# Last rows in blocks of 32, with narrower final matmuls, in a 2-D prefix-sum diagonal kernel

## The chip, the cores and the metric

One core of one Trainium2 chip. The metric is the device time of one execution in microseconds (us); lower is better. Executions of one kernel are compared with those of the other on the same chip.

## The reference

```python
B, H, W = 4, 4224, 4224                      # x: fp32
ps = np.cumsum(np.cumsum(x, axis=1), axis=2)
diag = np.diagonal(ps, axis1=1, axis2=2)
return np.cumsum(diag, axis=1).astype(np.float32)
```

All of x (285 MB) must be read; the output is small. An element counts once for every place of the diagonal at or beyond both its row and its column. Rows are summed on all engines, and weighted sums over the rows then give the output.

## The kernel before

Loads are issued by GpSimd, with a cast to bf16. VectorE masks and sums, ScalarE sums pieces of rows, TensorE adds columns and folds pieces of rows (with an identity as weights) into PSUM. The last 384 rows of the last matrix are done at the end: 256 rows "part a" in two cuts, then 128 rows "part b" in three cuts of columns. This is the tail that the change concerns:

```python
        acuts = [(1536, N - HC), (0, 1536)]          # part a, 256 rows
        bcuts = [(2432, TB), (640, 2432), (0, 640)]  # part b, 128 rows
        # ... loads are issued here, some 50 us ahead ...
        fold_in(fold_a, part_a, c0, cp, 256)         # second cut of part a, TensorE
        for h in range(2):
            act_sum(asum[:, h, 3:4], part_a[:, h, cp:c1])   # ScalarE
        row_sums(asum[:, :, 4], fold_a)              # VectorE
        row_sums(arows, asum)

        shares = [(768, 512), (768, 512), (0, 320)]
        for i, ((c0, c1), (wp, wa)) in enumerate(zip(bcuts, shares)):
            fold_in(fold_b, part_b, c0, c0 + wp, 256, start=i == 0)
            act_sum(tsum[:, n : n + 1], part_b[:, c0 + wp : c0 + wp + wa])
            # ... VectorE sums the rest of the cut, and at i == 2 fold_b ...
            if i == 0:
                matmul(fin_b, arows[:, 0:1], weights[:, 2 * P : GW], start=True)
                # ... three more of arows into fin_b and fin_a ...
        row_sums(ttot, tsum)
        matmul(fin_b, ttot, weights[:, 0:P])
        # ... two additions into yl, two stores ...
```

TensorE's records come in the order of the program: the folds of the first cut (660.49 us) go ahead of the matmuls of arows (661.37). And the waits of TensorE and VectorE in this tail are on data (the longest are 1.22 us of TensorE for ttot and 0.94 of VectorE for a landing).

## Time and profile before

| | before |
|---|---|
| time, first three runs | 668.81 us (668.69 to 669.55) |
| span of the profiled run | 667.0 us |
| load engines | 90% or more busy in 39 of 40 slices |
| VectorE, TensorE, ScalarE busy | 50%, 32%, 21% |
| last landing of part b to the issue of the last store | 1.62 us |
| that issue to the end of the span | 1.97 us |

The span is the profiler's, from the first to the last instruction; the time includes some 1.7 us more (668.75 us for the profiled run). The prediction below shows the lines of the page and of the timeline that carry this. A timeline line has start, duration, engine, source line, operation, output<-input, shape and count, and in brackets how long the engine had been idle and what ended that.

### The profile page before, as it was taken

What the parts mean: (1) busy time and instruction counts of PE and PEld (TensorE: products, weight loads), DVE (VectorE), ACT (ScalarE), POOL (GpSimd) and SP (SyncE); (2) the same over time, 40 slices, a digit from 0 to 9 for tenths busy, and PEclk for the clock granted to TensorE, in tenths of its full rate; (3) what the DMA queues carried; (4) which work ended last, traced back from release to release, by engine and by line L of the source; (5) the groups of instructions that cost most, each with busy time, mean ns of one, the idle gap of its engine ahead of it and who ended that gap; (6) DMA issues with size and microseconds to landing.
All of it is one profiled execution on the core that took longest, in us unless ns stands there. A gap on an engine that the chain in (4) does not pass through costs nothing.

```text
span 667.0 us, 2828 instructions
## 1 busy us (share of the span) xinstructions
PE 215.1 (32%) x967; PEld 97.2 (15%) x967; DVE 336.3 (50%) x376; ACT 140.1 (21%) x225; POOL 27.0 (4%) x56
## 2 busy tenths in 40 slices
PE   0071522403118254140321633504032254250426
PEld 0030211101003022010110311201011122120202
DVE  2043617366924351745883415266398241635687
ACT  0001120406300103040630020304063002030436
POOL 5000000000000000000000000000000000001000
PEclk9995857666558586665655957567565586765758
DMA  9999999999999999999999999999999999999997
GB/s 203 219 219 219 218 219 219 217 217 216 208 215 219 219 219 217 216 219 219 219 219 215 216 211 217 220 219 216 216 216 219 220 215 218 216 215 219 216 207 144
DMA packets 7384, 143.25 MB, mean 215 GB/s; under 512 B 669, under 2 KB 842, under 8 KB 1866
## 3 DMA queue, kind: packets, MB, share of 16 engines
q0 software_dynamic: 7008, 142.47, 99.7%
q1 hardware_dynamic: 362, 0.61, 0.3%
q8 instruction: 7, 0.11, 0.1%
q14 instruction: 7, 0.06, 0.0%
HBM read 285.47 MB, written 0.07 MB: 428 GB/s over the span
## 4 chain that ended last, share of the span: by engine, by line
another core or an unknown queue 42%; DVE 25%; PE 23%; DMA 5%; issue 4%; DVEq 0%; POOLq 0%
PE d L198 23%; DVE acc L215 17%; DVE mu L218 7%; DMA strip<-in_x_dram 5%; PE fold L198 1%; DVE pu L215 0%; DVE c L397 0%; DVE c L218 0%; DVE tsum L215 0%; DVE acc L301 0%; DVE acc L304 0%; PE carry_ps L198 0%; DVE rows L331 0%; DVEq L218 0%
## 5 line engine op out<-in xcount | busy, mean ns | idle before, releaser
L218 DVE SCALAR_TENSOR_TENSOR mu<-strip,um 128x768 bf16<-128x768 bf16 (+1 forms) x129 | 110.7, 908 | 314.4 <-DMA strip<-in_x_dram 222.3
L198 PE MATMUL d<-strip,sel 128*11 128x384 bf16 x603 | 140.0, 406 | 344.4 <-DMA strip<-in_x_dram 344.4
L210 ACT ACTIVATE dump<-strip 128x416 bf16<-128x416 bf16 (+8 forms) x112 | 128.4, 1146 | 523.2 <-DMA strip<-in_x_dram 520.2
L215 DVE TENSOR_REDUCE acc<-strip 128x6 f32<-128x4608 bf16 (+6 forms) x23 | 195.9, 8518 | 0.0
L198 PEld LDWEIGHTS <-sel 128*11 128x11 bf16 x849 | 86.1, 101 | 526.3 <-issue 488.4
L198 PE MATMUL d<-mu,sel 128*11 128x384 bf16 x243 | 59.7, 355 | 67.5 <-DVE mu L218 67.4
L75 POOL DMA_DIRECT2D strip<-in_x_dram x24 | 16.5, 687 | 555.5 <-DVE acc L215 414.5
L210 ACT ACTIVATION_READ_ACCUMULATOR dump<-strip 128x1 f32 x112 | 20.9, 186 | 0.0
L218 DVE DVE_READ_ACCUMULATOR mu<-strip,um 128x1 f32 x129 | 10.6, 82 | 0.0
L198 PE MATMUL d<-ident,rows 128*11 128x128 f32 x24 | 5.2, 378 | 16.5 <-DVE rows L340 16.5
L198 PE MATMUL fold<-strip,ident_h 128*128 128x480 bf16 (+1 forms) x14 | 4.3, 458 | 8.4 <-DMA strip<-in_x_dram 8.4
L198 PE MATMUL d<-halves,rows 128*11 128x64 f32 x48 | 5.7, 304 | 0.0
L198 PEld LDWEIGHTS d<-halves,rows 128*11 128x11 f32 x48 | 5.1, 136 | 2.1 <-issue 2.1
L198 PEld LDWEIGHTS d<-ident,rows 128*11 128x11 f32 x24 | 2.6, 118 | 18.2 <-DVE rows L340 11.5
L215 DVE TENSOR_REDUCE pu<-d 11x1 f32<-11x384 f32 x4 | 2.2, 546 | 5.5 <-PE d L198 5.5
L397 DVE TENSOR_TENSOR_SCAN c<-ones_row,carry,c 11x384 f32<-11x384 f32 x4 | 4.0, 1006 | 0.1
L397 DVE TENSOR_TENSOR_SCAN c<-ones_row,carry,d 11x384 f32<-11x384 f32 x4 | 4.0, 1001 | 0.1
L198 PEld LDWEIGHTS <-ident_h 128*128 128x128 bf16 x20 | 2.2, 112 | 12.2 <-issue 11.8
L215 DVE TENSOR_REDUCE parts<-strip 128x3 f32<-128x3072 bf16 x1 | 3.4, 3350 | 0.0
L198 PE MATMUL d<-hmu,sel 128*11 128x384 bf16 (+2 forms) x3 | 0.7, 286 | 6.7 <-DVE hmu L218 6.7
L372 POOL DMA_DIRECT2D strip<-in_x_dram x2 | 1.4, 716 | 29.2 <-DVE acc L215 29.2
L215 DVE TENSOR_REDUCE tsum<-strip 128x1 f32<-128x384 bf16 (+2 forms) x3 | 1.7, 568 | 0.9 <-DMA strip<-in_x_dram 0.9
(78 smaller groups left out, 36.0 us busy)
## 6 DMA issues: line engine op xcount, KB each, us to landing
strip<-in_x_dram POOLq DMA_DIRECT2D x19, 6336.0 KB, 69.6
strip<-in_x_dram POOLq DMA_DIRECT2D x5, 3168.0 KB, 55.3
strip<-in_x_dram POOLq DMA_DIRECT2D x1, 1080.0 KB, 45.3
strip<-in_x_dram POOLq DMA_DIRECT2D x1, 768.0 KB, 48.2
head<-in_x_dram SPq DMA_DIRECT2D x1, 528.0 KB, 3.9
strip<-in_x_dram POOLq DMA_DIRECT2D x1, 448.0 KB, 51.1
strip<-in_x_dram POOLq DMA_DIRECT2D x1, 416.0 KB, 49.5
strip<-in_x_dram POOLq DMA_DIRECT2D x1, 160.0 KB, 51.4
```

The lines of the kernel that those rows point to most:

```text
L75: nc.gpsimd.dma_start(out=o, in_=x[b, r0 : r0 + f * P, :].rearrange("(p f) w -> p f w", f=f))
L198: nc.tensor.matmul(o, lhsT=lhsT, rhs=rhs, start=start, stop=False, skip_group_check=True)
L210: nc.scalar.activation(out=dump[:, :w], in_=src, func=ACT.Copy, accum_out=acc)
L215: nc.vector.reduce_sum(out=acc, in_=src, axis=AX.X)
L218: nc.vector.scalar_tensor_tensor(out=o, in0=i, scalar=1.0, in1=m, op0=ALU.mult, op1=ALU.mult, accum_out=acc,)
L372: nc.gpsimd.dma_start(out=part_a[:, :, c0:c1], in_=src_a[:, :, c0:c1])
L397: nc.vector.tensor_tensor_scan(out=c12[:, i, :], data0=ones_row, data1=src, initial=carry[:, i : i + 1], op0=ALU.mult, op1=ALU.add,)
```

## The change

The intent is to shorten what follows the last landing. Part b comes in blocks of 32 rows, each row spread over four partitions. The last block then concerns only 32 places of the output, so the last matmuls and the last addition cover 32 instead of 128 columns, and each partial sum goes into PSUM by a matmul of its own, without an addition of sums first.

```diff
+    quarter = consts.tile([R, P], FP32, name="quarter")      # R = 32; mask made on GpSimd
+    w4_ps = psum_s.tile([P, P], FP32, name="fold")
+    matmul(w4_ps, quarter, weights[:R, :P], start=True)       # weights for quarter rows
...
-            bcuts = [(2432, TB), (640, 2432), (0, 640)]
-            for c0, c1 in bcuts:
-                nc.gpsimd.dma_start(out=part_b[:, c0:c1], in_=x[b, TB:N, c0:c1])
-            fold_a = psum_s.tile([P, 2, 256], FP32, name="fold_a")
+            for sb, c0, c1 in ((0,0,CB), (1,0,CB), (2,0,CB), (3,0,bcut), (3,bcut,CB)):  # CB = 1024, bcut = 640
+                r0 = TB + sb * R
+                nc.gpsimd.dma_start(out=part_b[:, sb, c0:c1],
+                    in_=x[b, r0 : r0 + R, :TB].rearrange("r (k c) -> r k c", k=4)[:, :, c0:c1])
+            fold_a = psum_s.tile([P, 2, P], FP32, name="fold_a")
...
+        weigh(arows[:, 0:1], weights, 0, fins, start=True)    # fins: fin_a 256, fin_m 96, fin_e 32 columns
+        weigh(arows[:, 1:2], weights, P, fins)
+        weigh(dtot, weights, M0, fins)                        # eight matmuls, ahead of all folds of part b
+        for sb, (wp, wa) in enumerate([(512, 512), (384, 384), (384, 320)]):
+            # folds of 128 columns into fold_b[:, sb], act_sum, and at sb == 0:
+                finish(fin_a, 0, M0)                          # VectorE addition
+            # VectorE sums the rest of the block
+        row_sums(bsum[:, :, 2], fold_b)
+        row_sums(btot, bsum)
+        for sb in range(3):
+            weigh(btot[:, sb : sb + 1], weights4, M0 + sb * R, fins)
+        # last block: four sums (two ScalarE, two VectorE) into esum
+        for k in range(4):
+            weigh(esum[:, k : k + 1], weights4, E0, fins)
+        finish(fin_m, M0, E0)       # store of 352 places
+        finish(fin_e, E0, GW)       # store of 32 places
```

## The prediction

> **What bounds the kernel now.** I read the page first: the load row by slices, then the chain that ended last.

> ```profile
> span 667.0 us, 2828 instructions
> DMA  9999999999999999999999999999999999999997
> GB/s 203 219 219 219 218 219 219 217 217 216 208 215 219 219 219 217 216 219 219 219 219 215 216 211 217 220 219 216 216 216 219 220 215 218 216 215 219 216 207 144
> another core or an unknown queue 42%; DVE 25%; PE 23%; DMA 5%; issue 4%; DVEq 0%; POOLq 0%
> ```

> The 16 DMA engines are at 90% or more in 39 of 40 slices and move about 217 GB/s of bf16, so the kernel is a stream of loads, and VectorE at 50% or TensorE at 32% follow it. The 42% of "another core or an unknown queue" is waiting for that stream. What a change of the last 128 rows can move is only what follows the stream: the last slice. So I then read the timeline from 658 us. Its columns are start, duration, engine, line, operation, output<-input, shape, and in brackets the idle time before and what ended it.

> ```profile
> 658.49 0.81 PE L198 MATMUL fold_a<-strip,ident_h 128*128 128x512 bf16 x3 [0.38 <-DMA strip<-in_x_dram]
> 660.30 0.66 DVE L215 TENSOR_REDUCE asum<-fold_a 128x2 f32<-128x512 f32 x1
> 660.49 0.49 PE L198 MATMUL fold<-strip,ident_h 128*128 128x256 bf16 x3 [1.19 <-DMA strip<-in_x_dram]
> 661.06 0.16 DVE L215 TENSOR_REDUCE arows<-asum 128x2 f32<-128x10 f32 x1
> 661.37 0.60 PE L198 MATMUL fin_b<-weights,arows 128*1 128x128 f32 x4 [0.39 <-DVE arows L215]
> 661.80 0.81 PE L198 MATMUL fin_a<-weights,arows 128*1 128x256 f32 x4
> 662.62 0.69 DVE L215 TENSOR_REDUCE tsum<-strip 128x1 f32<-128x512 bf16 x1 [0.94 <-DMA strip<-in_x_dram]
> 663.22 0.41 DVE L215 TENSOR_REDUCE tsum<-fold 128x1 f32<-128x256 f32 x1
> 663.51 0.47 ACT L210 ACTIVATE dump<-strip 128x320 bf16<-128x320 bf16 x1
> 663.55 0.47 DVE L215 TENSOR_REDUCE tsum<-strip 128x1 f32<-128x320 bf16 x1
> 664.13 0.16 DVE L215 TENSOR_REDUCE ttot<-tsum 128x1 f32<-128x8 f32 x1
> 664.35 0.38 PE L198 MATMUL fin_b<-weights,ttot 128*1 128x128 f32 x2 [1.22 <-DVE ttot L215]
> 664.77 0.28 DVE L446 TENSOR_TENSOR yl<-fin_b,c 1x128 f32<-1x128 f32 x1 [0.16 <-PE fin_b L198]
> ```

> The landings show as the starts after waits: the last cut of the rows before (a1) at 658.49, then the three cuts of the last rows at 660.49, 662.62 and about 663.5. From the last landing the path is: VectorE sum 0.47, ttot 0.16, final matmul 0.38, addition 0.28, store. The store is issued at 665.07 (its own record) and the span ends at 667.04, so 1.97 us follow that issue. The quantity to predict is when the last store is issued: 665.07 before.

> [...] packets of 1280, 3072, 3328 and 3584 bytes last 117, 248, 265 and 284 ns, about 24 ns plus 13.7 bytes per ns. [...] the trace has no row of bf16 matmuls of 128 columns with full weights (256 columns: 107 ns from start to start)[...]. [...] Here each VectorE record starts after the one ahead of it, even ttot, which waited.

> **Part by part.**
> Start: a mask of 32x128 on GpSimd (memset and two selects, some 0.7 us by its like there), one small matmul, one copy, one memset. GpSimd's constants end at 10.79 us and VectorE's at 8.8; the first strip lands at 34.6. Hidden, 0.

> Loads: three transfers become five; each partition takes 2048+2048+2048+1280+768 bytes instead of 3328+3584+1280. Each engine serves 8 partitions, so it has 16 packets more at 24 ns: 0.38 us, perhaps 0.34 because packets overlap a little (the DMA share reads 1.06 there). By the 8 packets of each engine, the landings should be at about a1 + 1.3, 2.6, 3.9, 4.8 and 5.4 us: 659.8, 661.1, 662.4, 663.3, 663.9. The last transfers reuse semaphores of earlier loads, which landed by 634.7, some 27 us before; the stream does not run dry.

> fold_a halves from 2x256 to 2x128 columns. TensorE streams the same columns (six matmuls of 256 instead of three of 512). Its VectorE sum drops from 0.655 to 0.414, the time of the 128x256 PSUM sum at 663.22: minus 0.24. arows is done at 660.98 instead of 661.22, and its first matmul can start at 661.13 instead of 661.37.

> Final matmuls of arows: eight logical fp32 matmuls now stand ahead of the folds of the last rows on TensorE; before, the first fold went ahead of them. Each is two passes of 0.84 ns per column (256 columns start 215 ns apart, 128: 108, 64: 54). Up to the one that completes fin_a: 2x(256+96+32)x0.84 = 0.645, then 0.108 to its second pass, plus 0.27 of that pass: done at 662.15. The other four, 2x256x0.84 = 0.43, let folds start at 662.42. [...] Between 0.054 each and 0.107 each this is 663.2 to 663.7.

> VectorE is the new path. Straight after arows its program has the addition that finishes fin_a, which waits for TensorE until 662.2; before, that addition filled the gap after ttot. VectorE thus stands idle 1.2 us, although the second block has landed at 661.1. Then: fin_a 0.32 (0.40 less 0.08 of overlap, as successive records show), bsum of 256 elements 0.32, bsum of 320 elements 0.39: 663.23. The sum of the fold (3x128 columns, 0.53 between 0.41 at 256 and 0.655 at 512) waits for TensorE: 663.47 to 664.00. Then 0.10 for its result, btot started at 664.10, esum of 320 at 664.18, esum of 256 at 664.57, ended at 664.98 (0.40). Next 0.05 to TensorE, two passes of 32 columns (0.03 and 0.19 to drain): 665.25; addition of 32 places 0.19: 665.48; store issued 665.50. The addition for fin_m and the first store fit beside the last matmuls.

> Sum: 665.50 - 665.07 = plus 0.43 us. What the change saves behind the last landing (ttot gone, addition of 32 instead of 128 places: 0.28 to 0.19; matmul record 0.38 to 0.22) is real but stands behind a VectorE that is late: the last block has landed 0.7 us before VectorE gets to it.

> **Rivals.**
> 1. The intended gain shows. If VectorE were free at 663.9, the path would be sum 0.40, matmul 0.27, addition 0.23, issue: about 664.9, minus 0.2 us, so 668.6. For it: the removed tail lies on the chain. Against it: the early fin_a addition and 1.5 us of VectorE work between the last fold and the last sum.
> 2. The loads become the bound: small pieces land later than I reckon. Against: packets' own durations give only 0.38 us, and 0.7 us of slack stand behind it. Were they 1.2 us late, the end would be 0.5 us later still, 669.7.
> 3. TensorE becomes the bound: weight loads of the folds not hidden, or its clock halved. The clock reads 1.00 from 656 to 664. [...]

> **Range and chances.** 668.81 + 0.43 gives 669.2. Runs of before spread over 0.86 us, and the working can err by some 0.6 us: 668.4 to 670.1. Two per cent is 13.4 us, twice the whole time after the last fold started; nothing touches the stream of loads ahead of that. Within 2%: 0.985, faster 0.005, slower 0.01.

> **What would show it.** In the changed profile: the load row as before; VectorE idle for over 1 us before the addition into yl from fin_a, released by TensorE; the fold sum at about 663.5 waiting for TensorE; the two esum sums on VectorE back to back without a wait for a load. Wrong if the last esum starts after a wait for a load (rival 2), if the sum of fold starts without waiting or well before 663.4 (towards rival 1), or if the stream before 650 us moves.

The sum came to plus 0.43 us (665.50 for 665.07). Passages that no trace of this case shows are cut where marked, and terms of that sum are among them: what one of the ten folds takes, and with it when they end and how much the third rival costs. What stays is the range for their end, 663.2 to 663.7, an estimate from the trace: ten times what 128 columns take at 0.42 ns (256 start 107 ns apart) or at twice that (480 start 400 ns apart at 650.4, where the clock reads 0.50), and some 0.2 us for the last to end (records of 256 columns last 270 ns). The sum took an end between the two, so that the fold sum starts at 663.47. From the range alone the estimate is plus 0.2 to 0.7. That VectorE keeps the order of its program rests on the trace: the addition of fin_a starts at 664.21, after ttot, though TensorE was done with fin_a at 662.62. In the records packets of 1280, 3072, 3328 and 3584 bytes last 116, 248, 267 and 286 ns, and each cut of part b is 128 packets (8 for each of the 16 load engines if they share evenly, as the forecast took it).

## The result

The changed kernel took 670.75 us (median of 6, 669.8 to 671.77); the kernel before, on the same chip, 669.28 (median of 6, 668.69 to 670.25). The ratio is 1.0021 with a 95% interval of 1.0008 to 1.0034. (Ratios here are the mean time of one kernel's fast runs over the mean of the other's in the same rounds, so not quite the ratio of the medians.) The change is slower by some 1.4 us where I had said 0.43, and 670.75 lies outside the range of 668.4 to 670.1. Both times are within 2% of each other, as forecast.

The page of the changed kernel, its first line and the load row: the stream is as it was.

```profile
span 669.0 us, 2916 instructions
DMA  9999999999999999999999999999999999999996
```

The timeline of the changed kernel, the tail, to set beside the lines of the prediction:

```profile
659.20 0.81 PE L214 MATMUL fold_a<-strip,ident_h 128*128 128x256 bf16 x6 [0.82 <-DMA strip<-in_x_dram]
660.57 0.39 DVE L236 TENSOR_REDUCE asum<-fold_a 128x2 f32<-128x256 f32 x1
661.18 0.16 DVE L236 TENSOR_REDUCE arows<-asum 128x2 f32<-128x10 f32 x1 [0.22 <-ACT dump L231]
661.40 0.66 PE L214 MATMUL fin_a<-weights,arows 128*1 128x256 f32 x2 [1.38 <-DVE arows L236]
...
662.29 0.61 PE L214 MATMUL fin_a<-weights,arows 128*1 128x128 f32 x2
...
662.95 0.41 DVE L480 TENSOR_TENSOR yl<-fin_a,c 1x256 f32<-1x256 f32 x1 [1.60 <-PE fin_a L214]
...
663.69 1.25 PE L214 MATMUL fold<-strip,ident_h 128*128 128x128 bf16 x10
...
664.98 0.56 DVE L236 TENSOR_REDUCE bsum<-fold 128x3 f32<-128x384 f32 x1 [0.90 <-PE fold L214]
665.64 0.16 DVE L236 TENSOR_REDUCE btot<-bsum 128x3 f32<-128x9 f32 x1
665.72 0.80 DVE L236 TENSOR_REDUCE esum<-strip 128x1 f32<-128x320 bf16 x2
...
666.83 0.18 DVE L480 TENSOR_TENSOR yl<-fin_e,c 1x32 f32<-1x32 f32 x1
667.05 0.25 SPq L516 DMA_DIRECT2D out_dram<-yl  x1
```

The shape is what I predicted: VectorE waits 1.60 us for fin_a, then 0.90 us for the folds, then works without a wait to the end. But TensorE is far slower than reckoned: from the first matmul of arows at 661.40 to the end of the folds at 664.94 it takes 3.54 us, where the range in the forecast gives 2.1 to 2.6. The next view says why. It gives for two stretches of 3.4 us the busy time (and number of instructions) of PE, PEld, DVE, ACT and POOL, then the granted TensorE clock, the share of the load engines and GB/s; first the kernel before, then the changed kernel:

```profile
658.40:661.80 3.40, 1.73 (x10) 0.84 (x10) 3.14 (x5) 2.59 (x6) 0.00 (x0) 1.00 0.98 189
661.80:665.20 3.40, 1.69 (x11) 0.62 (x8) 2.17 (x6) 1.28 (x4) 0.00 (x0) 1.00 0.08 13
```

```profile
658.40:661.80 3.40, 1.22 (x8) 0.66 (x9) 2.64 (x5) 2.49 (x6) 0.00 (x0) 1.00 1.10 200
661.80:665.20 3.40, 3.14 (x25) 2.35 (x23) 1.35 (x4) 2.24 (x10) 0.00 (x0) 0.50 0.23 40
```

The two profiles differ by 2.0 us of span. The last cut of part a lands at 658.49 before and at 659.20 after, 0.71 us later; from that landing to the issue of the last store it takes 6.58 us before and 7.85 after. So 1.27 us belong to the tail, and 0.71 to the stream of loads ahead of it. This is a comparison of one profile with one; the experiments show how little that is.

### The profile page after: what moved, and what is told of

Its sections match the earlier page's. It is cut to its first block, busy times and chain, and to the rows that moved or that the text cites. A ratio compares the mean times of both kernels' runs of the same rounds, so it can differ in the third digit from the quotient of the medians.

```text
span 669.0 us, 2916 instructions
## 1 busy us (share of the span) xinstructions
PE 216.3 (32%) x1005; PEld 99.9 (15%) x1005; DVE 336.8 (50%) x380; ACT 140.9 (21%) x229; POOL 28.0 (4%) x61
## 4 chain that ended last, share of the span: by engine, by line
another core or an unknown queue 37%; DVE 24%; PE 22%; DMA 13%; issue 4%; ACT 0%; DVEq 0%; POOL 0%; POOLq 0%; ACTq 0%
PE d L214 21%; DVE acc L236 16%; DMA strip<-in_x_dram 13%; DVE mu L239 6%; DVE pu L236 0%; PE fin_m L214 0%; DVE c L239 0%; ACT dump L231 0%; PE fold L214 0%; DVE acc L327 0%; DVE acc L324 0%; PE fin_a L214 0%; PE fin_e L214 0%; PE carry_ps L214 0%
## 5 line engine op out<-in xcount | busy, mean ns | idle before, releaser
L214 PE MATMUL d<-strip,sel 128*11 128x384 bf16 x603 | 138.6, 403 | 334.8 <-DMA strip<-in_x_dram 334.8
L231 ACT ACTIVATE dump<-strip 128x416 bf16<-128x416 bf16 (+9 forms) x114 | 129.1, 1132 | 523.1 <-DMA strip<-in_x_dram 520.2
L214 PE MATMUL fold<-strip,ident_h 128*128 128x128 bf16 (+1 forms) x18 | 4.6, 440 | 7.6 <-DMA strip<-in_x_dram 7.6
```

Source lines behind the costliest of these rows:

```text
L214: nc.tensor.matmul(o, lhsT=lhsT, rhs=rhs, start=start, stop=False, skip_group_check=True)
L231: nc.scalar.activation(out=dump[:, :w], in_=src, func=ACT.Copy, accum_out=acc)
```

## The experiments

**Theory, as first put.** The change moves the eight matmuls of arows ahead of the folds of part b. That leaves TensorE idle between the last fold of part a and arows (659.85 to 661.40), the clock drops at its next step, and folds that stand behind a slow stream of matmuls come late. **Rivals.** VectorE is blocked by the early addition of fin_a, as the prediction had it; the two further loads land late; the stream is delayed; the amount of work on VectorE is the bound. The first half of the theory (the new order is needed for the drop) fell in the course of the runs; the second half (what a drop costs) stood.

A look is one profiled run. The table has every look, the two first profiles included, ordered by where the clock's next possible step falls, with the three looks with fillers at the end. "Landing" is the start of the first fold on the last cut of part a. "Step" is how long after it the step of the 3.41 us grid falls (of the steps on that grid, the one from 1.0 to 4.4 us after the landing). "Tail" is from the landing to the issue of the last store.

| look | landing, us | step, us after it | clock halved there | tail, us |
|---|---|---|---|---|
| no folds, second | 658.61 | 1.46 | yes | 6.62 |
| changed, third | 660.12 | 1.63 | yes | 7.77 |
| before, fourth (state unknown) | 658.57 | 2.11 | yes | 7.57 |
| changed, fin_a's addition last | 659.60 | 2.11 | yes | 8.25 |
| before, arows first, third (unknown) | 659.98 | 2.16 | yes | 7.83 |
| changed, fold first, second | 658.45 | 2.33 | yes | 7.67 |
| changed, first | 659.20 | 2.60 | yes | 7.85 |
| before with the start part, second | 658.96 | 2.72 | yes | 7.28 |
| before, second | 658.47 | 3.09 | no | 6.58 |
| changed, second | 659.29 | 3.58 | no | 6.60 |
| before, third (unknown) | 658.52 | 3.67 | no | 6.58 |
| before, first | 658.49 | 3.93 | no | 6.58 |
| changed, fold first | 659.59 | 3.97 | no | 6.72 |
| no folds | 658.59 | 3.99 | no | 6.18 |
| before, arows first | 658.51 | 4.07 | no | 6.58 |
| before with the start part | 659.51 | 4.24 | no | 6.60 |
| before, arows first, second (unknown) | 658.60 | 4.27 | no | 6.58 |
| no folds, with fillers | 660.43 | 1.16 | no | 6.20 |
| changed, with fillers | 659.09 | 2.76 | no | 6.45 |
| before, with fillers | 658.86 | 2.85 | no | 6.58 |

**The changed kernel again** (no edit).

> The changed kernel once more, to see how much of its tail depends on where the TensorE clock's steps fall. In its first profile the clock went to 0.5 at 661.80 us, in the middle of the matmuls of arows, and the time from the end of arows (VectorE) to the issue of the last store was 5.71 us (kernel before: 3.85 us). Clock theory: where the clock stays at 1.00 through this stretch, that time is about 4.4 us, as the prediction worked it out; where it drops again, 5.5 to 5.8. Rival (order on VectorE and TensorE alone): 5.6 to 5.8 whatever the clock. Time against before: 1.002 again.

Its clock stayed at 1.00 to the end. From the end of arows to the last store 4.31 us instead of 5.71, and the tail was 6.60 us, that of the kernel before within 0.02. 670.06 us against 668.98 (ratio 1.0008, 0.9992 to 1.0024). From its timeline:

```profile
662.70 0.41 DVE L480 TENSOR_TENSOR yl<-fin_a,c 1x256 f32<-1x256 f32 x1 [1.13 <-PE fin_a L214]
663.04 0.73 PE L214 MATMUL fold<-strip,ident_h 128*128 128x128 bf16 x10
663.82 0.56 DVE L236 TENSOR_REDUCE bsum<-fold 128x3 f32<-128x384 f32 x1
...
665.89 0.25 SPq L516 DMA_DIRECT2D out_dram<-yl  x1
```

The same program, with the same order on every engine, has tails 1.25 us apart. The clock is the only difference found that can make the slow one slow (its arows even ended 0.15 us sooner after the landing). So the late folds of the first profile are put down to the clock, and at full clock the change costs 0.02 us in the tail. One thing more shows here: at full clock VectorE waits 1.13 us for fin_a, but not for the folds. What holds it up then is the early addition of fin_a, as the prediction had it; the folds hold it up only when the clock is halved.

**Fillers.** Matmuls whose result nobody reads:

```diff
         fold_in(fold_a, part_a, c0, cp, P)
+        warm = psum_d.tile([NG, GW], FP32, name="d")
+        for i in range(8):
+            matmul(warm, sel[:, :NG], part_a[:, 0, i * 8 : i * 8 + GW], start=i == 0)
```

> Eight idle-filling matmuls of 384 columns into an accumulator that nobody reads stand between the last fold of part a and the matmuls of arows, where TensorE was idle for 1.6 us. Clock theory: the clock stays at 1.00 to the end, the folds end some 1.2 us earlier (1.5 instead of 3.3 us after the first matmul of arows, less a little), and from the end of arows to the last store it takes about 4.4 us instead of 5.71: about 1.2 us less in the median. Rival (order alone): 5.6 us or more, the time unchanged.

From its timeline:

```profile
659.83 1.47 PE L214 MATMUL d<-strip,sel 128*11 128x384 bf16 x8
...
661.28 0.59 PE L214 MATMUL fin_a<-weights,arows 128*1 128x256 f32 x2
...
662.69 0.73 PE L214 MATMUL fold<-strip,ident_h 128*128 128x128 bf16 x10
663.46 0.56 DVE L236 TENSOR_REDUCE bsum<-fold 128x3 f32<-128x384 f32 x1
...
665.54 0.25 SPq L519 DMA_DIRECT2D out_dram<-yl  x1
```

The step fell at 661.85 us, all but where the clock dropped in the first profile (661.80), and it did not drop. (Counted from the landing it fell at 2.76, at the border of the looks that dropped, so the place alone might have spared it. By the rule below it would not have: in its stretch 2.49 us of columns streamed, far over the 1.28 of any that dropped, and 1.29 of them, 8 x 384 columns at 0.42 ns, are the fillers' own. An estimate from these: without them 1.2, just on the side that drops.) Ten folds take 0.73 us instead of 1.25, and from arows to the last store 4.31. With more work on TensorE the tail is 1.40 us shorter than in the first profile. 668.93 us against 668.98 for the kernel before (ratio 0.9994, 0.9981 to 1.0008). Against the changed kernel in the same job the mean is 0.84 us less (668.96 to 669.80, 95% interval 0.2 to 1.5; a comparison picked afterwards), so here the gain seems to show in the time too.

**The addition of fin_a moved.** `finish(fin_a, 0, M0)` goes from `sb == 0` to just ahead of `finish(fin_m, M0, E0)`.

> Only the addition that finishes fin_a moves on VectorE, from straight after arows to ahead of that of fin_m. My prediction's theory (VectorE blocked by that addition sets the end): VectorE sums the second block at about its landing, but fin_a's 0.32 us comes back on the end; gain at most 0.2 us. TensorE theory (the ten folds behind the matmuls of arows set when the fold sum can start): the fold sum starts as late as before, about 3.6 us after the end of arows when the clock drops, and the end is 0.3 us later than in the changed kernel. Neither makes it faster by over 0.2 us.

The clock dropped at 661.71. VectorE summed the second block at 662.07, at its landing, but the sum of the folds started as late as ever, 3.78 us after arows, and the addition's time came on top: 6.11 us from arows to the last store, 0.4 more than 5.71 where I had 0.3. The rival of the prediction (VectorE held up by that addition) is refuted while the clock is halved; the folds set the end. (669.1 us against 668.98; ratio 1.0006, 0.999 to 1.0022; its profiled run was the slowest of its six, 671.52.)

**Folds of the first block first.**

```diff
-        weigh(arows ...); weigh(arows ...); weigh(dtot ...)      # ahead of the loop
+            if sb == 0:  weigh(arows ...); weigh(arows ...); weigh(dtot ...)   # after the folds of block 0
```

> Only TensorE's order: the four folds of the first block go ahead of the matmuls of arows, as in the kernel before, in the 1.6 us in which TensorE stood idle. TensorE theory: 0.43 us less work (0.22 at full clock) between arows and the end of the folds, and TensorE is busy in the gap, so that the clock drops less often; from arows to the last store 4.2 us at full clock, 5.2 at half: 0.3 to 1.2 us less in the median. Rival (VectorE blocked by the addition of fin_a): no gain, since that addition waits as long as before.

The clock stayed at 1.00; 4.24 us from arows to the last store, tail 6.72. But its step up had fallen at 656.74 us, unlike the first profile's 654.97, so 3.97 us after the landing, and this look did not test the order where it matters. 669.97 us against 668.98 (ratio 1.001, 0.9996 to 1.0023): no gain in time was seen.

**The kernel before again** (no edit).

> The kernel before once more, for its profile. The last cut of part a landed at 658.47 us in its first profile, and at 659.06 to 659.58 in five profiles of the changed kernel and its variants. If the change itself delays the stream of loads, it lands at 658.6 or earlier again; if that is a difference from run to run, anywhere up to 659.6. From that landing to the last store 6.6 us either way (landing-bound), and the ratio of times is 1.000 within 0.0015.

Landing at 658.47, tail 6.58, 670.0 us against 669.92 (ratio 1.0004). Such an early landing fits a stream that the change delays; the runs with the start part, below, test that.

**The kernel before with fillers** (five of the same matmuls after its last fold of part a).

> The kernel before with five of the same idle-filling matmuls between its last fold of part a and its first fold of the last rows. Clock theory: the clock was 1.00 there anyway, so the time is the same (ratio 1.000 within 0.0015) and 6.6 us pass from the landing of the last cut of part a to the last store. Rival (fillers speed up any version, through something else than the clock of that stretch): 0.5 us or more faster.

Tail 6.58: fillers gain nothing against a look of the kernel before whose clock did not drop. 668.75 us against 669.92 (ratio 0.999, 0.9975 to 1.0005), inconclusive as a time.

**No folds.** Instead of the ten folds:

```diff
+        wa = CB // 2
+        for sb in range(3):
+            act_sum(bsum[:, sb, 0:1], part_b[:, sb, :wa])
+            if sb == 2:
+                finish(fin_a, 0, M0)
+            row_sums(bsum[:, sb, 1:2], part_b[:, sb, wa:])
```

> The changed kernel without its ten folds on TensorE: ScalarE and VectorE take half of each block of 1024 columns, and the addition that finishes fin_a stands between VectorE's second and third block. Theory (the folds behind the matmuls of arows set the end): the last sum on VectorE starts within 0.15 us of the last landing instead of 1.9 (half clock) or 0.6 (full clock) after it; from the last landing to the last store 1.0 to 1.1 us at full clock instead of 2.85 (half) or 1.58 (full); at half clock up to 1.6. About 1.2 us less than the changed kernel in the median, 0.2 to 0.5 less than the kernel before. Rival (VectorE's amount of work is the bound): it has 384 more elements to sum and 384 fewer to take from PSUM, so nothing gained.

Its timeline:

```profile
660.65 1.27 DVE L236 TENSOR_REDUCE bsum<-strip 128x1 f32<-128x512 bf16 x2
661.86 0.41 DVE L479 TENSOR_TENSOR yl<-fin_a,c 1x256 f32<-1x256 f32 x1
662.33 0.69 DVE L236 TENSOR_REDUCE bsum<-strip 128x1 f32<-128x512 bf16 x1
663.14 0.16 DVE L236 TENSOR_REDUCE btot<-bsum 128x3 f32<-128x6 f32 x1
663.22 0.83 DVE L236 TENSOR_REDUCE esum<-strip 128x1 f32<-128x320 bf16 x2
```

VectorE has no wait for TensorE left. The last sum starts at 663.63, at the last landing (663.62), and 1.14 us later the last store is issued. (I had 1.0 to 1.1.) So VectorE's amount of work was not the bound. But this edit does two things: it also moves the addition of fin_a from the first block to the third. At full clock, where the changed kernel did not wait for its folds, the shorter tail (6.18 against 6.60) can't be put down to the folds alone. As a time nothing is shown: 669.83 us against 669.92 (ratio 0.9999, 0.9984 to 1.0014), since 0.4 us are less than the runs' own spread of 2 us.

**No folds, with fillers** (eight before and eight after the matmuls of arows).

> The one before it with idle-filling matmuls on both sides of the matmuls of arows. Clock theory: full clock to the end, 1.0 to 1.1 us from the last landing to the last store, 0.3 to 0.6 us less than the kernel before in the median. If the folds alone were the cause and the clock does nothing here, the same time as without fillers.

1.15 us from the last landing, tail 6.20, the same as without fillers where the clock did not drop. 668.4 us against 669.92 (ratio 0.9988, 0.9974 to 1.0003), not clear of 1.

**One part of the change alone: the kernel before with arows first on TensorE.**

```diff
         for i, ((c0, c1), (wp, wa)) in enumerate(zip(bcuts, shares)):
+            if i == 0:  # the four matmuls of arows
             fold_in(fold_b, part_b, c0, c0 + wp, 256, start=i == 0)
...
-            if i == 0:  # the four matmuls of arows
```

> The kernel before with one thing of the change alone: on TensorE the matmuls of arows go ahead of the folds of the first cut of the last rows, which leaves TensorE idle from the last fold of part a until arows. Clock theory: where the clock's step at about 661.6 us falls as it did in the two slow profiles (a step up at 654.7 to 655.1), the clock drops to 0.5 there, and 7.6 to 7.9 us pass from the landing of the last cut of part a to the last store; where it does not drop, 6.6 as before, since one fold of 0.32 us more behind arows still ends about when the second cut lands. Rival (the drop comes from the smaller folds or the larger number of final matmuls): no drop, 6.6.

The step fell 4.07 us after the landing, nothing dropped, and the tail was 6.58. So this order costs nothing at full clock. Whether the clock drops more easily with it, the look did not test. Its six times fell in two groups, two at 668.8 and four at 670.5 to 671.2 (median 670.73 against 669.16; ratio 1.001, 0.9994 to 1.0027). Three more:

> The changed kernel a third time, on the same chip as the others here. From the landing of the last cut of part a to the last store: about 6.6 us if the clock stays at 1.00 between 661 and 665 us, 7.8 or more if it drops. Ratio to the kernel before between 1.0005 and 1.0025.

Dropped at 661.75, tail 7.77. 670.86 us against 669.16 (ratio 1.0019, 1.0002 to 1.0036).

> The changed kernel with the folds of the first block ahead of the matmuls of arows, a second time, for another fall of the clock's steps. Clock theory: full clock through the matmuls of arows, and 6.4 to 6.8 us from the landing to the last store, whatever the fall of the steps, because TensorE streams for 1.3 us or more in the 3.41 us before the step. If the clock drops here too, the gap on TensorE isn't what decides it.

This one missed: I had expected no drop. The clock dropped at 660.78, in the middle of the matmuls of arows, and the tail was 7.67. In the 3.41 us ahead only 1.00 us of matmul columns had streamed; most of arows came after the step. With the order of the kernel before on TensorE, the changed kernel dropped all the same. 669.91 us (ratio 1.0009).

> The version without folds again, beside the changed kernel on the same chip. From the landing of the last cut of part a to the last store 6.2 us at full clock (1.15 from the last landing); about 6.6 to 7.0 if the clock drops, since its matmuls of arows then end late but no fold stands behind them. Median 0.3 to 1.3 us below the changed kernel, 0.0 to 0.6 below the kernel before.

The clock dropped at 660.07, and the tail was 6.62, as expected, against 7.77 of the changed kernel: without folds behind arows a halved clock costs 0.44 us, not 1.2. 669.07 us (ratio 0.9995, 0.998 to 1.0009); against the changed kernel in the same job the mean is 1.6 us less (669.14 to 670.78, 95% interval 0.4 to 2.9, picked afterwards too).

What was left open was whether order alone brings the drop. Four more looks, not timed (one run each, so their state is unknown; they came from one chip):

> The order-only kernel a second time. If the step up falls at 653.9 to 655.1 us: order theory, a drop at 660.8 to 661.9, and 7.6 us or more from the landing of the last cut of part a to the last store (two folds of 256 columns more behind a matmul stream at half speed); rival (the rest of the change is needed), no drop and 6.6. At another fall of the steps without a drop between 660 and 662: 6.6 either way.

Step 4.27 us after the landing, no drop, tail 6.58.

> The order-only kernel a third time, with the same expectation: 7.6 us or more from that landing to the last store if the clock drops between 660 and 662 us (order theory: it does so when the step up falls at 653.9 to 655.1), 6.6 if not.

The clock dropped at 662.14, and the tail was 7.83 us.

> The kernel before a third time. Order theory: no drop between 661 and 665 us at a step up of 654.7 to 655.6 (1.6 us of matmuls in the 3.41 us ahead of it), 6.6 us from the landing to the last store. If a step falls earlier (at 660 to 661 us) it may drop; then the cost is under 0.4 us, since its first folds already stand ahead of arows and the loads set the end.

No drop, tail 6.58. The step up of these last two lay 0.05 us apart (655.31 and 655.36), and for a while I took them for the proof that order brings the drop. They are not: the landing was at 659.98 in the one and at 658.52 in the other, so the step fell 2.16 us into the tail here and 3.67 there.

> The kernel before a fourth time, with the same expectation: 6.6 us from the landing to the last store without a drop, at most 7.0 with one.

A miss, and the most useful look. With the step 2.11 us after the landing, the kernel before dropped too, at 660.68, and its tail was 7.57 (I had allowed 7.0). Its stretches before and after that step, columns as above:

```profile
657.26:660.68 3.42, 1.16 (x9) 0.65 (x10) 2.87 (x6) 2.17 (x7) 0.00 (x0) 1.00 1.07 211
660.68:664.09 3.41, 3.41 (x14) 1.24 (x12) 1.31 (x3) 1.87 (x6) 0.00 (x0) 0.50 0.39 73
```

TensorE is about as little busy ahead of the step as in the changed kernel (1.16 and 1.22 us), and the clock behind it is halved alike. So the order of the change is not needed for a drop.

**The start part of the change alone: the kernel before with the mask, its matmul and the copy.**

```diff
+    quarter = consts.tile([R, P], FP32, name="quarter")      # memset and two selects on GpSimd
+    w4_ps = psum_s.tile([P, P], FP32, name="fold")
+    matmul(w4_ps, quarter, weights[:R, :P], start=True)
+    weights4 = consts.tile([P, P], FP32, name="weights4")    # copied on VectorE, read by nobody
```

> The kernel before with only the start of the change: the mask on GpSimd, the small matmul, the copy into weights4, and the SBUF that they take; nothing reads weights4. Theory that the start delays the stream: the first strip lands at 35.8 us or later (35.0 before) and the last cut of part a at 659.2 or later, ratio about 1.001. Rival (spread from run to run): first strip at about 35.0, part a at 658.5 to 658.7, ratio 1.000 within 0.0015. The tail from that landing is that of the kernel before in either case, 6.58 or 7.6 us.

Landing at 659.51, a microsecond later than in the four looks of the kernel before (658.47 to 658.57). The step fell 4.24 us after it, the tail was 6.60. 669.5 us against 669.57 (ratio 1.0002, 0.9989 to 1.0015). One oddity: this trace's clock reads 0.85 where the others read 1.00.

> The same kernel a second time, since one look at the landing can't tell a delay of 0.6 us from a spread of as much: the same expectation, and the two together should agree.

Landing at 658.96, the step 2.72 us after it, and a second drop in a kernel with the old tail. From its timeline, against the prediction's lines of the kernel before:

```profile
658.96 0.81 PE L212 MATMUL fold_a<-strip,ident_h 128*128 128x512 bf16 x3 [0.79 <-DMA strip<-in_x_dram]
...
661.89 1.48 PE L212 MATMUL fin_a<-weights,arows 128*1 128x256 f32 x4
...
664.17 0.42 DVE L234 TENSOR_REDUCE tsum<-fold 128x1 f32<-128x256 f32 x1 [0.40 <-PE fold L212]
...
665.93 0.28 DVE L465 TENSOR_TENSOR yl<-fin_b,c 1x128 f32<-1x128 f32 x1 [0.36 <-PE fin_b L212]
```

The matmuls into fin_a take 1.48 us instead of 0.81, and VectorE, which did not wait for the folds before, waits 0.40 us for them, and 0.36 instead of 0.16 for the last matmul. 669.64 us against 669.57 (ratio 1.0003, 0.9989 to 1.0016).

Both looks landed later than the kernel before did, the first as the theory of a delayed stream expected, the second (658.96) between its 659.2 and the rival's 658.7; both ratios fit the rival (1.000 within 0.0015). In these looks the delay begins early. The load rate from 6 to 8 us, the kernel before, then this one (last column GB/s):

```profile
6.00:8.00 2.00, 0.00 (x0) 0.00 (x0) 2.00 (x8) 0.00 (x0) 1.79 (x11) 1.00 1.24 266
```

```profile
6.00:8.00 2.00, 0.00 (x0) 0.00 (x0) 0.41 (x2) 0.00 (x0) 1.79 (x12) 1.00 0.73 152
```

(The eight looks without the start part moved 215 to 266 GB/s there, the ten of the changed kernel and its variants 165 to 266.) The first strip landed at 36.76 and 36.57 us in these two looks and at 34.97 to 36.79 (mean 35.84) in the ten others with the start part, against 34.64 to 35.53 (mean 35.01) in the eight looks without it. But nothing that the start part adds runs before 10.04 us, when the rate had long fallen behind. A rival stands: these two looks ran on a chip on which no other look is known to have been taken. And a late landing comes without the start part too (659.98, arows first, third). And as a time the start part is not shown to cost anything (1.0002 and 1.0003). A later landing is seen; its cause, its mechanism and its price are not shown.

**One rule for all looks.** For each whole stretch of 3.41 us between possible steps, from the last step up ahead of the landing to the first drop after it, I summed how long matmul columns stream in it: 0.42 ns per bf16 column and 0.84 ns per fp32 column and pass (256 columns start 107 and 215 ns apart at full clock in the first profile of the kernel before). The 20 profiles give 58 stretches. All 19 that end in a drop have 1.28 us or less; all 39 that don't have 1.30 or more. The two sides all but touch, so the border is near 1.29, and a sum within some hundredths of it says nothing. This border was found at the tail, but it holds for the whole of the 20 traces. Of 1033 stretches at full clock, the 407 that end in a drop have 1.24 us or less but for one (1.28), and the 626 that don't have 1.26 or more. At half clock a column takes twice the time (480 bf16 columns start 400 ns apart in that profile at 650.4 us, 0.83 ns each); counted as if at full clock, the 2254 stretches there that end without a step up have 1.34 us or less, and the 387 that end in one 1.34 or more but for one (1.29). In the first profile of the changed kernel the stretch ahead of the drop has 1.04 us; in that of the kernel before, the stretch with the same work has 1.49; with fillers in the changed kernel it is 2.49; in the kernel before where it dropped (its fourth look) 0.76, and with the start part 1.28.

By this rule, and the records of each kernel at full clock, I slid the stretch along the tail. An estimate from these durations, with the border at 1.26 to 1.29: a drop follows when the step falls 1.15-1.55 to 2.8-3.2 us after the landing in the kernel before (three looks), and 1.4 to 3.0 us in the changed one (one look). That is some 1.6 us of 3.41 for either. With arows first alone it is 1.15 to 3.1, some 1.95 us: the order by itself would make a drop likelier, but the changed kernel as a whole is not likelier to drop by this estimate. The drop costs it more. With a drop the tail of the changed kernel is 1.17 and 1.25 us longer than without (7.77 and 7.85 against 6.60), that of the kernel before 0.99 longer, and 0.70 with the start part (7.28 against 6.58); without folds 0.44 (6.62 against 6.18).

**Where the 1.4 us are.** The means of the looks: the landing is 658.75 us in the eight looks without the start part, 659.29 in the twelve with it (0.5 later); the tail is 7.41 in three looks of the changed kernel (7.85, 6.60, 7.77) and 6.83 in four of the kernel before (6.58 three times, 7.57), 0.6 longer. Together 1.1 us, beside 1.4, 0.5 and 1.3 us (ratios 1.0021, 1.0008, 1.0019) in the three jobs that timed the two. The sizes are alike, but that is no proof. The 0.6 us of the tail come from a drop in two of three looks against one of four, and that may be luck: if both dropped in 1.6 of 3.41 falls, as estimated, their mean tails would differ by only some 0.1 us. That the halves add up to the 1.4 us is not shown.

**What stays open.** How the 1.4 us divide. How often the steps fall badly for each kernel: two of three looks of the changed kernel, one of four of the kernel before, which is no rate. Whether a later landing makes drops more frequent: the last step up before the tail lay between 654.7 and 655.4 us in ten of the twenty looks, so that two steps of 3.41 us on it is 661.5 to 662.2: 3.0 to 3.7 us after a landing at 658.5, but 2.3 to 3.0, in the bad stretch, after one at 659.2. Plausible, not shown. And why the first loads are slower with the start part. The times of the kernel before alone spread by up to 2.85 us in one job (668.55 to 671.4), of which a dropped clock explains 1.0. No version was shown to beat both kernels: the one without folds has the shortest tail (6.18 to 6.62), but its three ratios, 0.9999, 0.9988 and 0.9995, are none of them clear of 1.

## Why the prediction was wrong

In the pair of first profiles the span grew by 2.0 us where 0.43 were predicted. Of the excess, 0.84 us came in the tail (7.85 us against 6.58 plus 0.43), from the step named fifth below, and 0.71 from a later landing, which the prediction did not have.

- **The stream bounds the kernel, and the change plays only in the tail:** right. The load row is the same.
- **Added constants are hidden, 0:** on their engines they are: in the first profile the mask, the matmul, the copy and the memset are done by 12.4 us, and the first strip lands at 36.8. But the kernels with them land 0.5 us later in the mean, which I had not looked for. Not proved to be their doing, above.
- **Two more transfers cost 0.34 us:** wrong, but harmless. From the landing of part a to the last landing it took 4.96 us before and 5.00 to 5.08 after, 0.07 us more. The packets' own durations in the first profile (173 ns for 2048 bytes, 79 for 768) fit the forecast's 24 ns plus 13.7 bytes per ns, but they don't simply add up: their sum is 1.10 of the load engines' time from 658.40 to 661.80, so they overlap. The last two transfers were issued at 620.69 and 635.59, each 0.3 us after an earlier load had landed, and the share of the load engines stayed at 1.09 (658 to 660) and 1.12 (to 661.5). VectorE had slack there, as said.
- **fold_a's smaller sum gives 0.24 us:** its sum shrank as said (0.655 to 0.389), but in both slow profiles of the changed kernel arows had to wait for ScalarE and ended 2.14 us after the landing; in the one at full clock it ended 2.29 us after it. I had 2.49, reckoned from one profile of the kernel before (2.73); its other three looks have 2.32, 2.33 and 2.61. The gain has no fixed size.
- **Matmuls of arows, "done at 662.15", and folds "start at 662.42":** this is the step that failed. It counted every column at the full clock, because "the clock reads 1.00 from 656 to 664" in the one profile before. That reading is a matter of where the steps fell in that run: another look of the same kernel has 0.50 from 660.68. From the first matmul of arows to fin_a I reckoned 1.02 us; 1.03 were measured at full clock, 1.50 and 1.86 when it dropped. To the end of the folds 2.1 to 2.6 by the range in the forecast; 2.14 at full clock, then 3.54 and 3.46. The term missing from the sum is a drop in some runs, 1.2 us for the changed kernel and 0.7 to 1.0 for the kernel before.
- **Folds between 54 and 107 ns each:** the sum took a value between, an estimate that no trace showed. Measured 57 ns at full clock and 104 at half in the mean (0.73 and 1.25 us for ten, less the last one's drain), close to the two ends of the range. So at full clock the sum of the folds started without a wait for them, one of the signs that I had named for being wrong.
- **From the sum of the folds to the last store 2.03 us:** 2.07 in both. VectorE's chain, the idle wait for fin_a and the two esum sums back to back were right.
- **Sum:** 4.52 us from arows to the last store predicted, 4.31 measured at full clock, 5.71 and 5.63 with the drop. The 0.41 us by which the tail at full clock is shorter than predicted are this 0.21 and the 0.20 of an arows that ended earlier (2.29 for 2.49). Counted from the landing of part a, the tail at full clock is 0.02 us longer than before, where I had 0.43; when the clock drops in both, 0.2 to 0.3 us longer (7.77 and 7.85 against 7.57). So most of the 0.6 us by which the mean tail is longer comes from the larger share of looks in which the changed kernel dropped.
- **Rivals:** the third, "or its clock halved", was the nearest, set aside on that one reading. The size given for it (reckoned from the same cost of a fold) was too small as well: it slowed only the folds, not the fp32 matmuls ahead of them, and the sum of the folds came 1.5 us later than my 663.47, 0.36 of it because arows ended later (661.34 for 660.98).
- **Range:** it allowed 0.6 us for the working. A cost that comes in some runs and not in others, and a stream whose landing differs by 2 us between looks (658.45 to 660.43), needed about twice that.

## What to carry to other kernels

A clock read in one profile belongs to that run: in the kernel before it read 1.00 from 656 to 664 us in the first look and 0.50 from 660.68 in the fourth. Where matmuls are sparse, look at several profiles of the same kernel, note where the clock's steps fall in the work, and compare only looks in which they fall alike, before an effect is put down to an order of instructions. And keep work that others wait for off the engine whose speed is in doubt: without the ten folds, and with fin_a's addition later, a halved clock cost 0.44 us instead of 1.2.
